# Retention in a two-layer hybrid trunk: chunk states of a head pair as diagonal blocks of a 128-column tile

## The chip, the cores and the metric

The kernel runs on one core of a Trainium2 chip. The metric is device time in microseconds (us). A core has a matrix engine, TensorE (PE), three engines that work on tiles of up to 128 partitions, VectorE (DVE), ScalarE (ACT) and GpSimd (POOL), and SyncE (SP), which here does nothing but issue DMAs. Each engine runs its own list of instructions in order; semaphores tie the lists together.

## The reference

Two layers of a diffusion trunk, 128 context tokens and 1024 latent tokens, width 1024. In each layer one projection feeds four mixers (retention, a Fourier mixer, latent attention, a Hyena convolution), whose outputs go through an output projection and a gated feed-forward network. The change is in the retention of the latent tokens, for four heads with 64 columns each, forward and backward, in chunks of 128 tokens:

```python
scores = jnp.einsum('bnchd,bnmhd->bnhcm', qc, kc) * dmask[None, None]
inner = jnp.einsum('bnhcm,bnmhe->bnche', scores, vc)
kv = jnp.einsum('bnchd,bnche->bnhde', kc * zeta[None, None, :, :, None], vc)
def step(S, kv_j):
    return g_chunk[None, :, None, None] * S + kv_j, S
s_final, s_prev = lax.scan(step, s0, kv)
cross = jnp.einsum('bnchd,nbhde->bnche', qc * xi[None, None, :, :, None], s_prev)
return (inner + cross).reshape(B, L, H, dv), s_final
```

`s_prev` holds the state of a head, 64 x 64, ahead of each chunk. The outputs of both directions are added, normed over a head's 64 columns and gated.

## The kernel before

Tokens lie in nine tiles of 128: eight latent ones and the context. A layer runs in phases: phase 1 (input projection and Hyena), phase 2 (Fourier mixer, retention, attention), phase 3 (output projection), feed-forward network. The layers' phases stand in the trace at about 550 to 840 us (end of phase 1 and phase 2 of layer 0) and 2280 to 2560 us (of layer 1).

A scheduler of the framework sets the order. It takes instructions as their operands and buffers come free, by priorities that the program gives: the Fourier mixer is ahead of the retention's preparation, and the heads' loads of attention are ahead of both. Buffers come from pools. A new pool takes the place of closed pools of an earlier phase, and its first writer waits for the last use there. PSUM, the accumulator memory of PE, is dealt out by tag in phase 2: two banks for transposes (`tr`), three for attention scores (`sc`), one for attention's output (`po`), two for the retention (`r`).

The retention goes through these steps:

- `ret_rope` (L1027) loads the rotation tables (`ropeR`) and q and k of all nine tiles from DRAM (`rqk`, from the projection's output `pj`), and rotates the eight latent tiles on DVE, with two instructions of 128 x 256 and two of 128 x 512 for each tile. The tile of chunk states, `Sall`, serves as scratch.
- `ret_tables` (L977) works out decay masks (`rD`), key scales (`rzt`), chunk decays (`rgt`) and query scales (`rxi`), many small instructions on DVE and ACT.
- `ret_states` (L1042) scales the keys of each tile (`rkz`, DVE), multiplies them with v (`rv`) on PE (L1061, output `pskv`), copies the 64 x 64 blocks on the diagonal into `Sall` (ACT, L1070), and runs the scan: 14 steps of a multiply and an add on DVE, each step on both head pairs at once.
- `ret_tile` (L1080), for each tile: transposes of q and k, scores of the four heads (L1099), their mask (L1100, `rsT`), then the output. For each head (64 columns): one inner product with the 128 rows of `rsT` (L1106) and two cross products, one for each direction, with the 64 rows of the head in `rqx` (scaled q) and `Sall` (L1109). Heads that lie on different halves of the 128 rows write different banks, so there are two output banks and two copies on ACT (L1110).
- `ret_group` (L1112) takes three tiles, then the norm and the gate for all three.

In phase 2 the attention calls `beside` after each pair of query tiles, which runs one step of `ret_group`: retention tiles lie between attention pairs on all engines. An attention pair is: scores on PE (L129 to L131, `sc`), a pass over them on DVE that frees the bank (L903, `pr`), the exponential on ACT (L906), transposes on PE (L917), their split into two parts on ACT and DVE (L120, L125), products with v on PE (L934, L935).

The pools of phase 2, in this order: `rp` (two buffers a tag, for the tiles), `rk` (one buffer, for what lives through the retention: `ropeR`, `Sall`, `rqk`, tables, `rv`), `fp` on the other side of the memory (Fourier), then `at` and `hd` (attention).

Of the kernel before, what the change touches and what calls it, by code (L numbers as in the profile page):

```python
# [10 lines left out]
F32 = mybir.dt.float32  # L11
F32R = mybir.dt.float32r
I32 = mybir.dt.int32
AF = mybir.ActivationFunctionType
ALU = mybir.AluOpType
AX = mybir.AxisListType
PSUM = bass.MemoryType.PSUM
# [18 lines left out]
# ---------------------------------------------------------------- constants of the shapes  # L36
def shape_constants():
# [33 lines left out]
    # channel and position DFTs of the Fourier mixer  # L71
# [10 lines left out]
    # rotary tables, [token of the tile, tile, (first half, second half)]  # L82
# [8 lines left out]
    # retention: distances, masks (with the key scale), positions  # L91
# [7 lines left out]
# ---------------------------------------------------------------- kernel  # L99
class Kern:  # L100
# [12 lines left out]
    # -- small helpers  # L113
# [19 lines left out]
    def rsqrt(self, y, v, pool, tag):  # L133
        """y = v ** -0.5, [p, n]"""
# [20 lines left out]
    # -- two engines for plain arithmetic  # L155
# [13 lines left out]
    # ------------------------------------------------------------ hyena: filters  # L169
    # slots of a tile spectrum (value = re - i * im)  # L170
# [3 lines left out]
    def dft_odd(self, z, d, s, y, tmp):  # L174
        """odd classes from z0, z4 ([p, 1, c]), d, s ([p, 3, c])"""
# [20 lines left out]
    def dft_even_sum(self, a, y, uv, e, s0=8):  # L196
        """classes 0, 8, 4 from a[t] = x[t] + x[t+4]  ([p, 4, c])"""
# [6 lines left out]
    def dft_even_diff(self, b, y, fe, e, s0=8):  # L204
        """classes 2, 6 from b[t] = x[t] - x[t+4]  ([p, 4, c])"""
# [12 lines left out]
    def fft_class(self, r, y, ps, cons, inverse):  # L218
        """ps [p, 2, c]: (re, im) of class r; cons [p, 3, 128]: cos, sin, -sin"""
# [13 lines left out]
    def first(self, n):  # L233
        """what follows n instructions earlier"""
        return self.tc.high_priority(offset=n) if n else nullcontext()

    # ------------------------------------------------------------ modulation rows
# [16 lines left out]
    def ada_steps(self, l, c0, n, pool, psp, tag, dve=(0, 1)):  # L254
        """modulation rows of layer l from column c0 on, n columns at a time, as steps to do beside other work:
        w * silu(c) summed over k-tiles, then over partitions"""
# [40 lines left out]
    # ------------------------------------------------------------ rms norm, modulation, transposition  # L297
    def rstd(self, junk, x, n):
        """1 / sqrt(mean(x^2) + EPS) of [p, n]"""
# [8 lines left out]
    def norm_mod(self, t, x, y, ra, rb, psp, tag, r=None, e="g"):  # L308
        """tile t of the modulated norm of x, transposed and split into T"""
# [21 lines left out]
    # ------------------------------------------------------------ hyena filters  # L331
    def sin_rows(self, v, k, ps, bias, out):
        """out = sin(ps + bias) with the argument brought into [-pi, pi]"""
# [12 lines left out]
    def filter_mlp(self, h1p, h2p, psp, tag):  # L346
        """hidden rows of the filter networks of both layers (64 rows each), to DRAM; the second copy runs backwards"""
# [27 lines left out]
    def filter_spectrum(self, l, o, p1, p2, psp, tag):  # L375
        """spectrum of filter o of layer l, to DRAM"""
# [44 lines left out]
        # the direct term: the filter at distance 0, before the division by the norm  # L421
# [30 lines left out]
    # ------------------------------------------------------------ hyena: long convolution  # L452
    ORDER = (0, 8, 4, 1, 3, 7, 5, 2, 6)

    def spec_mul(self, ps, G, p2):
        """(re, im) of ps * G, values re - i im"""
# [11 lines left out]
    def long_conv(self, l, o, z, gate, p1, p2, psp, tag):  # L468
        """z = gate * conv(z), [p, 9, 256] (tile 8: context); the direct term is part of the filter"""
# [43 lines left out]
        # the parts of the way to the spectrum, and of the way back, in time for the classes that need them  # L513
# [75 lines left out]
    # ------------------------------------------------------------ input projection, hyena, filters  # L589
    WC = 288  # L590

    def w_chunks(self, wp, src, c0, n):
        """weights [p, 8, cols] of columns c0.., four chunks of two k-tiles -> [(hi, lo)] per k-tile"""
# [11 lines left out]
    def hu_block(self, l, b, wp, h1p, sp, psp, ztile, xg):  # L605
        """128 channels of the hyena input: projection, short convolution, back to token rows"""
# [435 lines left out]
    def ret_states(self, l, zt, gt, Sall, keep, psp):  # L1042
# [4 lines left out]
        for d in range(2):  # L1047
            nc.sync.dma_start(Sall[:, 7 * d, :, d], A["sret"][l, :, :, d])
# [817 lines left out]
```

## Time and profile before

| | us |
|---|---|
| median of 3 runs | 3522.32 |
| lowest, highest | 3521.51, 3538.58 |
| profiled execution, its span | 3531.2 |
| PE busy | 3206.7 (91%) |
| DVE busy | 2700.7 (76%) |
| ACT busy | 1286.5 (36%) |
| POOL busy | 1122.7 (32%) |

The profile is of one execution, a little longer than the median. The busy shares are means over stages with different limits, so the stage that a change touches is read by itself: from the table by stretches (busy time of each engine, the granted clock of PE as a share of full speed), from the groups of one tile (count, durations, first and last start) and from the timeline (start, duration, instruction, and in brackets the idle time before it with what ended it). A product in fp32 stands in the trace as two passes. Passes overlap in the pipeline, so their own durations are longer than the distance between starts.

### The profile page before, as it was taken

How to read it: one execution, taken by the hardware profiler on the slowest of the kernel's cores; microseconds unless marked ns; L12 is line 12 of the kernel's file. 1: busy time of each engine (PE TensorE's matmuls, PEld its weight loads, DVE VectorE, ACT ScalarE, POOL GpSimd, SP SyncE). 2: the span in 40 equal slices, each digit the busy share in tenths (PEclk: the TensorE clock that was granted, in tenths of full speed). 3: DMA queues.
4: the chain of work that ended last, by engine and by line, in shares of the span. 5: the costliest groups of instructions: out<-in, count | busy, mean ns of one | idle time of the engine just before them, and what ended most of it. 6: DMA issues, size and time to landing. Idle time of an engine off the chain costs nothing.

```text
span 3531.2 us, 52713 instructions
## 1 busy us (share of the span) xinstructions
PE 3206.7 (91%) x18934; PEld 2830.7 (80%) x18934; DVE 2700.7 (76%) x5024; ACT 1286.5 (36%) x2496; POOL 1122.7 (32%) x947
## 2 busy tenths in 40 slices
PE   8899888999879999989968998899996999999897
PEld 5768777888779999967747787798885999998775
DVE  6676796767898888898897627666788866668898
ACT  3123113545444444443323232254544322223332
POOL 2111430001255555546661014201012422223664
PEclk8899899889989999999987999998898999999998
DMA  5454455104333344343223534531143322213223
GB/s 209 131 168 131 142 157 181 50 17 149 117 111 118 117 129 119 96 134 113 91 88 126 158 108 132 181 106 34 33 165 108 104 74 74 74 58 110 96 72 135
DMA packets 323349, 398.50 MB, mean 113 GB/s; under 512 B 60266, under 2 KB 253543, under 8 KB 322576
## 3 DMA queue, kind: packets, MB, share of 16 engines
q1 hardware_dynamic: 261312, 338.16, 30.1%
q10 hardware_dynamic: 61776, 56.97, 5.2%
q8 instruction: 150, 2.46, 0.3%
q14 instruction: 111, 0.91, 0.1%
HBM read 303.03 MB, written 92.00 MB: 112 GB/s over the span
## 4 chain that ended last, share of the span: by engine, by line
PE 55%; DVE 23%; DMA 6%; issue 6%; POOL 5%; ACT 4%; SPq 0%; ACTq 0%; DVEq 0%; POOLq 0%
PE gu L129 8%; PE gu L131 8%; PE gu L130 8%; DVE ho L125 3%; PE acc L131 3%; PE acc L130 2%; PE acc L129 2%; DMA adw<-in_wada 2%; DVE rq_w L146 2%; DVE acc L157 1%; DVE dw L125 1%; PE pstr L917 1%; DVE adacc L160 1%; POOL acc L157 1%; PE psr L1109 1%
## 5 line engine op out<-in xcount | busy, mean ns | idle before, releaser
L129 PE MATMUL dq<-dw,ho 128*128 128x512 f32 x704 | 289.3, 412 | 47.0 <-DVE acc L157 17.9
L131 PE MATMUL dq<-dw,ho 128*128 128x512 f32 x704 | 289.2, 411 | 34.9 <-DVE ho L125 34.7
L129 PE MATMUL gu<-X,fw 128*128 128x256 f32 x1024 | 290.1, 286 | 7.9 <-ACT fw L120 4.4
L160 DVE SCALAR_TENSOR_TENSOR adacc<-adw,csilu,adacc 128x256 f32<-128x256 f32 x392 | 239.7, 638 | 71.1 <-DMA adw<-in_wada 70.2
L131 PE MATMUL gu<-X,fw 128*128 128x256 f32 x1024 | 287.1, 283 | 1.8 <-DVE fw L125 1.8
L130 PE MATMUL dq<-dw,ho 128*128 128x512 f32 x704 | 287.1, 408 | 0.3 <-DVE dw L125 0.2
L130 PE MATMUL gu<-X,fw 128*128 128x256 f32 x1024 | 285.9, 282 | 0.0
L130 PE MATMUL acc<-wlo,Th 128*128 128x256 f32 (+1 forms) x720 | 217.4, 303 | 5.6 <-DVE wlo L125 5.6
L129 PE MATMUL acc<-whi,Th 128*128 128x256 f32 (+1 forms) x720 | 219.4, 307 | 0.0
L131 PE MATMUL acc<-whi,Tl 128*128 128x256 f32 (+1 forms) x720 | 215.8, 301 | 0.0
L129 PEld LDWEIGHTS dq<-dw,ho 128*128 128x128 f32 x704 | 138.2, 196 | 88.1 <-issue 41.6
L129 PEld LDWEIGHTS gu<-X,fw 128*128 128x128 f32 x1024 | 193.1, 190 | 18.6 <-ACT fw L120 8.1
L131 PEld LDWEIGHTS dq<-dw,ho 128*128 128x128 f32 x704 | 138.1, 196 | 78.3 <-DVE ho L125 45.4
L157 POOL TENSOR_TENSOR adacc<-adacc,adp 128x256 f32<-128x256 f32 x168 | 153.7, 915 | 131.4 <-ACT adp L272 124.4
L131 PEld LDWEIGHTS gu<-X,fw 128*128 128x128 f32 x1024 | 193.3, 190 | 2.3 <-DVE fw L125 2.3
L130 PEld LDWEIGHTS gu<-X,fw 128*128 128x128 f32 x1024 | 193.7, 190 | 0.0
L120 ACT ACTIVATE ho<-hraw 128x384 fp32r<-128x384 f32 (+1 forms) x192 | 87.8, 489 | 272.4 <-POOL hraw L157 254.7
L129 PE MATMUL gu<-x1s,fw 128*128 128x320 f32 x576 | 178.8, 310 | 3.6 <-DVE u L157 3.1
L131 PE MATMUL gu<-x1s,fw 128*128 128x320 f32 x576 | 179.5, 312 | 2.1 <-DVE fw L125 2.0
L130 PE MATMUL gu<-x1s,fw 128*128 128x320 f32 x576 | 179.0, 311 | 0.0
L125 DVE TENSOR_TENSOR ho<-hraw,ho 128x384 fp32r<-128x384 f32 (+1 forms) x192 | 165.6, 879 | 8.1 <-ACT ho L120 8.0
L130 PEld LDWEIGHTS dq<-dw,ho 128*128 128x128 f32 x704 | 138.3, 196 | 32.9 <-DVE dw L125 1.2
(526 smaller groups left out, 10186.7 us busy)
## 6 DMA issues: line engine op xcount, KB each, us to landing
adw<-in_wada SPq DMA_DIRECT2D x320, 128.0 KB
h<-U SPq DMA_DIRECT2D x176, 128.0 KB
X<-in_wf SPq DMA_DIRECT2D x42, 512.0 KB
fr<-in_wf SPq DMA_DIRECT2D x40, 512.0 KB
b<-in_wf SPq DMA_DIRECT2D x24, 768.0 KB
hraw<-h SPq DMA_DIRECT2D x24, 768.0 KB
pj<-pst ACTq DMA_DIRECT2D x90, 128.0 KB
G<-gt SPq DMA_DIRECT2D x36, 256.0 KB
```

Source lines behind the costliest of these rows:

```text
L120: nc.scalar.activation(hi, src, AF.Copy)
L125: (nc.vector if elo == "dve" else nc.gpsimd).tensor_tensor(out=lo, in0=src, in1=hi, op=ALU.subtract)
L129: mm(ps, lh, rh, start=start, stop=False)
L130: mm(ps, lh, rl, start=False, stop=False)
L131: mm(ps, ll, rh, start=False, stop=stop)
L146: nc.vector.scalar_tensor_tensor(out=w, in0=a, scalar=a[:, 0:1], in1=v, op0=ALU.mult, op1=ALU.mult)
L157: (self.nc.vector if e == "v" else self.nc.gpsimd).tensor_tensor(out=out, in0=a, in1=b, op=op)
L160: self.nc.vector.scalar_tensor_tensor(out=out, in0=a, scalar=s, in1=b, op0=op0, op1=op1)
L917: T(pst[:, j], pr[i][:, (k0 + j) * P:(k0 + j + 1) * P], self.ident)
L1109: nc.tensor.matmul(pi[:, pr], qx[q, pr, d], Sall[q, t, pr, d], start=False, stop=d == 1)
```

## The change

The states of a head pair become one 128 x 128 tile: head 0 in the upper left block, head 1 in the lower right, zeros in the other two. `Sall` grows from 64 to 128 columns for each chunk, pair and direction (8 to 16 KB a partition). One cross product then takes all 128 rows of scaled q and gives 128 columns, both heads of a pair; the heads share one output bank, and one copy of 256 columns follows. The zeros are set by two memsets on GpSimd, the loads of the start states go in halves (2 to 4 DMAs a layer), and the scan works on whole 128 x 128 blocks, one instruction for a pair and step (multiply and add in one; 28 a layer as before). To make room, `kvc` and `rv` move from the pool `rk` to tags of `rp` (`rv` gets two buffers, shared with the tiles' `rvg`), and `rot` has two buffers in place of four.

```diff
-        Sall = keep.tile([P, 8, 2, 2, 64], F32, name="Sall")
+        Sall = keep.tile([P, 8, 2, 2, P], F32, name="Sall")
...
-        kvc = keep.tile([P, 2, 2, 64], F32, name="kvc")
+        kvc = pool.tile([P, 4, P], F32, name="kvc", tag="rqkT")[:, 0:2].rearrange("p a (b e) -> p a b e", b=2)
         kzs = keep.tile([P, 2, 2, 4, 64], F32, name="rkz", tag="ropeR")
+        for hh in range(2):
+            nc.gpsimd.memset(Sall[64 * hh:64 * hh + 64, :, :, :, 64 - 64 * hh:P - 64 * hh], 0.0)
         for d in range(2):
-            nc.sync.dma_start(Sall[:, 7 * d, :, d], A["sret"][l, :, :, d])
+            for hh in range(2):
+                q = slice(64 * hh, 64 * hh + 64)
+                nc.sync.dma_start(Sall[q, 7 * d, :, d, q], A["sret"][l, q, :, d])
...
-                v3 = keep.tile([P, 3, 256], F32, name="rv")
+                v3 = pool.tile([P, 3, 512], F32, name="rv", tag="rvg")[:, :, 0:256]
...
-                        nc.scalar.activation(Sall[q, dst, :, d], ps[q, :, d, q], AF.Copy)
+                        nc.scalar.activation(Sall[q, dst, :, d, q], ps[q, :, d, q], AF.Copy)
...
-                tmp = keep.tile([P, 2, 64], F32, name="rst")
-                self.tt("v", tmp, Sall[:, prev, :, d], gt[:, :, d:d + 1].broadcast_to([P, 2, 64]), ALU.mult)
-                self.tt("v", Sall[:, t, :, d], Sall[:, t, :, d], tmp, ALU.add)
+                for k in range(2):
+                    self.stt(Sall[:, t, k, d], Sall[:, prev, k, d], gt[:, k, d:d + 1], Sall[:, t, k, d], ALU.mult, ALU.add)
...
-        for e in range(2):
-            q = slice(64 * e, 64 * e + 64)
-            pi = psp.tile([P, 2, 64], F32, name="psr", tag="r")
-            for pr in range(2):
-                h = 2 * pr + e
-                nc.tensor.matmul(pi[:, pr], sT[:, h], vg[:, 64 * h:64 * h + 64], start=True, stop=not lat)
-                if lat:
-                    for d in range(2):
-                        nc.tensor.matmul(pi[:, pr], qx[q, pr, d], Sall[q, t, pr, d], start=False, stop=d == 1)
-            nc.scalar.activation(o[:, e::2], pi, AF.Copy)
+        pi = psp.tile([P, 4, 64], F32, name="psr", tag="r")
+        for pr in range(2):
+            both = pi[:, 2 * pr:2 * pr + 2].rearrange("p h e -> p (h e)")
+            if lat:
+                nc.tensor.matmul(both, qx[:, pr, 0], Sall[:, t, pr, 0], start=True, stop=False)
+            for h in (2 * pr, 2 * pr + 1):
+                nc.tensor.matmul(pi[:, h], sT[:, h], vg[:, 64 * h:64 * h + 64], start=not lat, stop=not lat)
+            if lat:
+                nc.tensor.matmul(both, qx[:, pr, 1], Sall[:, t, pr, 1], start=False, stop=True)
+        nc.scalar.activation(o, pi, AF.Copy)
...
-            rt = pool.tile([P, 2, P], F32, name="rot", bufs=4)
+            rt = pool.tile([P, 2, P], F32, name="rot")
...
-                self.ret_states(l, zt, gt, Sall, rk, psp)
+                self.ret_states(l, zt, gt, Sall, rk, rp, psp)
```

The scratch of the rotations and tables in `Sall` moves to other chunks of it, since each is now twice as large. The order of the engines changes at the end of phase 1 and in phase 2 of both layers and nowhere else.

SyncE in layer 0, around the load of the rotation tables, before. `fin`, `fch`, `ffc`, `fcons` belong to the Fourier mixer, `rdec` and `rpos` to the decay tables:

```order
L290 DMA mod_5_251<-adw 2x256
L1031 DMA ropeR<-in_ropeR 128x1024
L1153 DMA fin<-pj_97 128x9x256
L1155 DMA fch<-in_chan 128x384
L1157 DMA ffc<-in_fouC 128x256
L1168 DMA fcons<-in_fouF 128x384 x2
L1036 DMA rqk<-pj_97 128x3x512 x3
L981 DMA rdec<-in_rdec 128x8
```

The same place after (`qn` and `kn` are the loads of an attention head):

```order
L1158 DMA fin<-pj_97 128x9x256
L1160 DMA fch<-in_chan 128x384
L1162 DMA ffc<-in_fouC 128x256
L1173 DMA fcons<-in_fouF 128x384 x2
L875 DMA qn<-qd_1250 128x864
L1173 DMA fcons<-in_fouF 128x384 x3
L1031 DMA ropeR<-in_ropeR 128x1024
L1036 DMA rqk<-pj_97 128x3x512 x3
L981 DMA rdec<-in_rdec 128x8
```

`ropeR` has moved behind all Fourier loads. What it waits for has changed too: before, stores and a copy of the Hyena mixer; after, the store and the copy of the last projection group (L732, L733) in layer 0, and in layer 1 those of a group with three still to come. The rest of the queue stands behind it.

DVE in layer 0, the first rotations (`Sall<-rqk,ropeR` and the three after it), before:

```order
L160 SCALAR_TENSOR_TENSOR fin<-fab 128x256 x4
L1188 TENSOR_TENSOR fab<-psx,fq 128x128
L157 TENSOR_TENSOR Sall<-rqk,ropeR 128x8x32 x3
L157 TENSOR_TENSOR rqk<-rqk,ropeR 128x512
L157 TENSOR_TENSOR Sall<-rqk,ropeR 128x8x32
L157 TENSOR_TENSOR rqk<-rqk,Sall 128x512
L1188 TENSOR_TENSOR fab<-psx,fq 128x128
L157 TENSOR_TENSOR rqk<-rqk,ropeR 128x512
```

DVE in layer 0, the end of the rotations and the first score row of attention (`pr,mx<-sc`), after:

```order
L157 TENSOR_TENSOR Sall<-rqk,ropeR 128x8x32
L157 TENSOR_TENSOR rqk<-rqk,Sall 128x512
L157 TENSOR_TENSOR rqk<-rqk,ropeR 128x512
L988 TENSOR_SCALAR rt_5472<-rt_5471 128x8
L997 TENSOR_SCALAR rt_5470<-rdec 128x8
L157 TENSOR_TENSOR rqk<-rqk,Sall 128x512
L989 RECIPROCAL rt_5472<-rt_5472 128x8
L903 TENSOR_SCALAR pr,mx<-sc 128x384
```

Before, the rotations stood between steps of the Fourier mixer, and tables, key scaling and the first scan steps came ahead of the first score row. After, the rotations follow the Fourier mixer as one block and the first score row comes right behind them, the tables (`rt`) beside the score rows, and the key scaling and the scan later, behind two pairs of attention. In layer 1 twelve attention rows stand ahead of the block.

PE in layer 0, the output products of the first retention tile, before:

```order
L1106 MATMUL psr<-rvg,rsT 128x64
L1109 MATMUL psr<-Sall,rqx 128x64 x2
L1106 MATMUL psr<-rvg,rsT 128x64
L1109 MATMUL psr<-Sall,rqx 128x64 x2
L934 MATMUL po<-pth,vhl 128x256
L1106 MATMUL psr<-rvg,rsT 128x64
L1109 MATMUL psr<-Sall,rqx 128x64 x2
L1106 MATMUL psr<-rvg,rsT 128x64
L1109 MATMUL psr<-Sall,rqx 128x64 x2
```

And after:

```order
L1110 MATMUL psr<-Sall,rqx 128x128
L1112 MATMUL psr<-rvg,rsT 128x64 x2
L1114 MATMUL psr<-Sall,rqx 128x128
L1110 MATMUL psr<-Sall,rqx 128x128
L1112 MATMUL psr<-rvg,rsT 128x64 x2
L1114 MATMUL psr<-Sall,rqx 128x128
```

Twelve products of 64 columns have become eight, the four cross ones with 128 columns; each shows as two passes.

## Rows read from the trace of the kernel before

**Rows 1.** The page: span, busy time of engines, one costly group (mean ns).
```profile
span 3531.2 us, 52713 instructions
...
PE 3206.7 (91%) x18934; PEld 2830.7 (80%) x18934; DVE 2700.7 (76%) x5024; ACT 1286.5 (36%) x2496; POOL 1122.7 (32%) x947
...
L160 DVE SCALAR_TENSOR_TENSOR adacc<-adw,csilu,adacc 128x256 f32<-128x256 f32 x392 | 239.7, 638 | 71.1 <-DMA adw<-in_wada 70.2
```

**Rows 2.** Table by stretches: busy time and instructions, then clock and DMA.
```profile
core 0: us, PE busy (x) PEld busy (x) DVE busy (x) ACT busy (x) POOL busy (x), PEclk, DMA share, GB/s
597.00:645.00 48.00, 41.06 (x254) 35.23 (x252) 39.15 (x128) 31.21 (x85) 1.28 (x1) 0.93 0.39 114
645.00:800.00 155.00, 148.51 (x894) 134.71 (x894) 95.27 (x274) 74.67 (x153) 14.81 (x11) 0.82 0.09 24
2280.00:2345.00 65.00, 63.63 (x478) 59.55 (x478) 38.68 (x111) 24.48 (x69) 0.00 (x0) 1.00 0.50 157
2345.00:2384.00 39.00, 37.95 (x283) 35.38 (x281) 31.46 (x104) 25.33 (x64) 1.27 (x1) 1.00 0.33 93
2384.00:2545.00 161.00, 154.00 (x966) 139.98 (x965) 102.79 (x299) 79.95 (x162) 16.28 (x12) 0.86 0.11 30
```

**Rows 3.** Groups of tile psr: ns min/median/max, first and last start.
```profile
L1109 PE MATMUL psr<-Sall,rqx x256: 272/272/473, 645.4 to 2528.8; 64*128 64x64 f32 x128
...
L1087 PE MATMUL psr<-ident,rqk x72: 272/273/273, 635.8 to 2534.2; 128*128 128x128 f32 x72
...
L1110 ACT ACTIVATE ro<-psr x36: 277/278/278, 647.1 to 2537.7; 128x128 f32<-128x128 f32 x36
```

**Rows 4.** Timeline of PE, half of layer 0's first tile: start, duration.
```profile
645.08 0.43 PE L1106 MATMUL psr<-rvg,rsT 128*128 128x64 f32 x2
645.44 0.66 PE L1109 MATMUL psr<-Sall,rqx 64*128 64x64 f32 x4
646.03 0.43 PE L1106 MATMUL psr<-rvg,rsT 128*128 128x64 f32 x2
646.39 0.66 PE L1109 MATMUL psr<-Sall,rqx 64*128 64x64 f32 x4
646.98 0.38 PE L934 MATMUL po<-pth,vhl 128*128 128x256 f32 x1
```

**Rows 5.** Timeline of PE, kv products of layer 0.
```profile
599.68 1.64 PE L1061 MATMUL pskv<-rv,rkz 128*128 128x128 f32 x12
```

**Rows 6.** Timelines of SyncE and of ACT's DMA queue: issues.
```profile
550.94 0.35 SPq L1031 DMA_DIRECT2D ropeR<-in_ropeR  x1
...
556.00 0.40 SPq L1036 DMA_DIRECT2D rqk<-pj  x1
...
596.21 0.33 ACTq L733 DMA_DIRECT2D pj<-pst  x1
...
2342.18 0.33 ACTq L733 DMA_DIRECT2D pj<-pst  x1
```

**Rows 7.** Groups of tiles rqk, Sall and rkz on DVE (both layers).
```profile
L157 DVE TENSOR_TENSOR Sall<-rqk,ropeR x32: 396/414/440, 573.5 to 2302.4; 128x256 f32<-128x256 f32 x32
L157 DVE TENSOR_TENSOR rqk<-rqk,ropeR x16: 674/682/710, 574.5 to 2302.8; 128x512 f32<-128x512 f32 x16
L157 DVE TENSOR_TENSOR rqk<-rqk,Sall x16: 676/682/703, 575.4 to 2303.6; 128x512 f32<-128x512 f32 x16
L157 DVE TENSOR_TENSOR rkz<-rqk,rzt x36: 404/420/426, 599.1 to 2367.4; 128x256 f32<-128x256 f32 x36
L157 DVE TENSOR_TENSOR rst<-Sall,rgt x28: 272/282/837, 598.7 to 2382.5; 128x128 f32<-128x128 f32 x28
```

**Rows 8.** Timelines of DVE and PE: first rotation, rv wait, first score rows.
```profile
573.46 0.77 DVE L157 TENSOR_TENSOR Sall<-rqk,ropeR 128x256 f32<-128x256 f32 x2
...
610.45 4.58 PE L1061 MATMUL pskv<-rv,rkz 128*128 128x128 f32 x24 [2.37 <-DMA rv<-pj]
...
614.72 0.55 DVE L903 TENSOR_SCALAR_CACHE_REDUCE pr<-sc 128x384 f32<-128x384 f32 x1
...
2351.57 0.56 DVE L903 TENSOR_SCALAR_CACHE_REDUCE pr<-sc 128x384 f32<-128x384 f32 x1
```

More of the change, by code (lines that the diff above doesn't have):

```diff
@@ L1010, in ret_tables @@
         nc.scalar.activation(gt, lt, AF.Exp, scale=float(P))
-        scratch = Sall[:, 4:8].rearrange("p t a b c -> p (t a b c)").rearrange("p (n c) -> p n c", c=P)
+        scratch = Sall[:, 4:6].rearrange("p t a b c -> p (t a b) c")
         dist, tm, prow = scratch[:, 0:4], scratch[:, 4:6], scratch[:, 6:8]
@@ L1037, in ret_rope, with ret_states @@
             if t < CTX:
-                tmp = Sall[:, 2 * (t % 2):2 * (t % 2) + 2].rearrange("p a b c d -> p (a b c) d")
+                tmp = Sall[:, t % 2].rearrange("p b c (e d) -> p (b c e) d", d=64)
                 self.rope("v", self.qk[:, t].rearrange("p (h d) -> p h d", h=8), tabs[:, :, t], tmp, 8, 64)
         return Sall
-    def ret_states(self, l, zt, gt, Sall, keep, psp):
+    def ret_states(self, l, zt, gt, Sall, keep, pool, psp):
         nc, A = self.nc, self.A
-        kvc = keep.tile([P, 2, 2, 64], F32, name="kvc")
+        kvc = pool.tile([P, 4, P], F32, name="kvc", tag="rqkT")[:, 0:2].rearrange("p a (b e) -> p a b e", b=2)
         kzs = keep.tile([P, 2, 2, 4, 64], F32, name="rkz", tag="ropeR")
+        for hh in range(2):
+            nc.gpsimd.memset(Sall[64 * hh:64 * hh + 64, :, :, :, 64 - 64 * hh:P - 64 * hh], 0.0)
         for d in range(2):
-            nc.sync.dma_start(Sall[:, 7 * d, :, d], A["sret"][l, :, :, d])
+            for hh in range(2):
+                q = slice(64 * hh, 64 * hh + 64)
+                nc.sync.dma_start(Sall[q, 7 * d, :, d, q], A["sret"][l, q, :, d])
         for t in range(NT):
             if t % 3 == 0:
-                v3 = keep.tile([P, 3, 256], F32, name="rv")
+                v3 = pool.tile([P, 3, 512], F32, name="rv", tag="rvg")[:, :, 0:256]
                 nc.sync.dma_start(v3, self.proj[l][:, t:t + 3, 768:1024])
@@ L1087, in ret_tile @@
             nc.tensor.transpose(ps[:, j], self.qk[:, t, j * P:j * P + P], self.ident)
-        qkT = pool.tile([P, 4, P], F32, name="rqkT")
+        qkT = pool.tile([P, 4, P], F32, name="rqkT", tag="rqkT")
         nc.scalar.activation(qkT, ps, AF.Copy)
@@ L1100, in ret_tile @@
             nc.vector.tensor_tensor(out=sT[:, e::2], in0=pe[e], in1=Dm[:, e::2], op=ALU.mult)
-        for e in range(2):
-            q = slice(64 * e, 64 * e + 64)
-            pi = psp.tile([P, 2, 64], F32, name="psr", tag="r")
-            for pr in range(2):
-                h = 2 * pr + e
-                nc.tensor.matmul(pi[:, pr], sT[:, h], vg[:, 64 * h:64 * h + 64], start=True, stop=not lat)
-                if lat:
-                    for d in range(2):
-                        nc.tensor.matmul(pi[:, pr], qx[q, pr, d], Sall[q, t, pr, d], start=False, stop=d == 1)
-            nc.scalar.activation(o[:, e::2], pi, AF.Copy)
+        pi = psp.tile([P, 4, 64], F32, name="psr", tag="r")
[8 more added lines that the diff above has]
+        nc.scalar.activation(o, pi, AF.Copy)
     def ret_group(self, l, g, Dm, xi, Sall, pool, psp):
         nc = self.nc
-        vg = pool.tile([P, 3, 512], F32, name="rvg")
+        vg = pool.tile([P, 3, 512], F32, name="rvg", tag="rvg")
         o = pool.tile([P, 12, 64], F32, name="ro", bufs=1)
```

## Prediction

> **What bounds the kernel now.** I read the page first: TensorE (PE) is busy for 91% of the span of 3531.2 us, VectorE (DVE) for 76%, ScalarE for 36% [rows 1]. That average says little about the stage that the change touches, so the next view is a table by stretches [rows 2]. In both layers the change lies in the end of phase 1 and in phase 2. In the long middle of phase 2 (645 to 800 us in layer 0, 2384 to 2545 in layer 1) PE is busy for 148.5 of 155 us and 154.0 of 161, DVE for 95.3 and 102.8: PE sets the pace there, and its granted clock is only 0.82 and 0.86 of full speed. In the stretch before (597 to 645) PE has 41.1 of 48 us and DVE 39.2; in layer 1 (2345 to 2384) PE 38.0 of 39 and DVE 31.5. So at the start of phase 2 neither has much room, and in the middle what PE is relieved of is worth its time, until DVE (61 to 64% there) comes close. Before 2345 PE is full (63.6 of 65) and DVE is not (38.7): there DVE work costs nothing.
>
> **The products of a tile.** A latent tile takes 24 passes (an fp32 product shows as two): 8 inner ones with 128 rows and 16 cross ones with 64 rows, both 64 columns wide. In the timeline [rows 4] half a tile runs from 645.08 to 646.98: 1.90 us for 12 passes, 3.80 for a tile. The next work on the list is other work, so this is all that the tile costs PE once its operands are there. After, there are 8 inner and 8 cross passes, 128 rows each, cross 128 columns wide. The nearest row for these is the kv product, 128 rows and 128 columns: 12 passes in 1.64 us [rows 5], and a lone record of that width lasts 0.272 [rows 3], so a pass every (1.64 - 0.27) / 11 = 0.125 us. 16 x 0.125 = 2.0 us, 1.8 less for a tile; 16 latent tiles (8 in each layer) give **-29 us**. Upper bound of the gain: the inner passes, half as wide, at half of it, 16 x 2.3 = -37. Lower bound: nothing, if a 128-column pass costs two of the old ones.
>
> Do two 64-row passes share the array today? The four of one head start at 645.44 and the next product at 646.03, so 0.15 us each, one behind the other [rows 4]. "TensorE: Matmul & The Clock Gate" of the Trainium skill (Part 3, and its table of what to do with small matmuls) says that products on different row groups can run at the same time in the array. By that rule one 128-row product would replace two that might have shared a slot, and the sum would have nothing for the 16 tiles; but the kernel before puts the passes of one row group together, and the rows show no sharing. It is a rival below, with a small chance.
>
> **The clock.** The two stretches with retention tiles run at 0.82 and 0.86, the two stretches of layer 1 before them at 1.00 [rows 2]. Lost against full speed: 155 x 0.18 = 28 us and 161 x 0.14 = 22 us, 50 in all. What differs is that half-filled products stand in the one kind of stretch and not in the other; wide 128-row products replace them. Bounds: -50 if the clock stays at full speed, 0 if it falls as before. I take the half, **-25**: some of the lost cycles lie in the very products that shrink (counted above), and some low stretches follow idle PE, which stays.
>
> **The start of phase 2.** The tile of states (Sall) grows from 8 to 16 KB a partition, and the pool that holds it with the rotation tables (ropeR) and q and k (rqk) can now only be placed on buffers of phase 1. Before, SyncE issued ropeR at 550.94 us and the first rqk at 556.00, and the rotations ran on DVE from 573.46, beside the last projection products [rows 6, 8]. In the new order ropeR stands behind the storing of the last projection group in layer 0, and behind a group with three still to come in layer 1 (that is what its semaphores lead to); everything that SyncE issues later (rqk, decay tables, rv, the next heads' q and k) queues behind it. The groups' stores were issued at 596.21 and 2342.18 [rows 6]. From there to the first rotation: a store, a table, 768 KB of rqk. No row shows this alone; from rqk's issue to the first rotation it was 17.5 us with other work between, which is the upper end, zero the lower; I take 8. The rotations of a layer are 16 x 0.414 + 8 x 0.682 + 8 x 0.682 = 17.5 us of DVE [rows 7], in one block ahead of the first score row of attention in layer 0, and behind a dozen of those in layer 1.
> Layer 0: 596 + 8 + 17 = 621 us for the first score row, against 614.72 before [rows 8], 6 late. The kv products that PE did before 614.72 now come behind two pairs of attention, some 48 of 72 passes at 0.137 [rows 5], another 7: **+13**. Layer 1: 2342 + 8 = 2350, when the projection ends too; the first score row came at 2351.57 before [rows 8] and comes about then again, a dozen such rows take 5 us, and then the 17 us of rotations hold back all others. PE has scores and transposes for some 5 of these: **+12**. Bounds for a layer: +5 (only the wait, with attention work beside the rotations) and +35 (wait, rotations and a third of the next block with an idle PE).
>
> **Tables, states, scan.** The table arithmetic moves between attention rows, where DVE has room. The key scaling (18 x 0.42 = 7.6 us) and the scan (28 x 0.282 = 7.9) [rows 7] stood among the attention rows; in the new order the scan is one unbroken block ahead of the first tile. The instructions stay 28, now a scalar-tensor-tensor of 128 x 128; the nearest row is 128 x 256 at 0.638 [rows 1], half of that 0.32, so 1 us more a layer. While the block runs no score leaves its bank; PE has kv products and transposes for part of it. Between 0 and 16 us a layer, I take 5: **+10**. Costed at nothing: the two memsets on GpSimd, hidden by the rotations' wait and the key scaling, which come first (uncovered, they would hold the scan back by some us); two more DMAs for the start states, beside the same work; ScalarE's copy of the output, one of 256 columns for two of 0.278 [rows 3], on an engine that is 36% busy; rot with two buffers for four, where ScalarE waits for a store at each third copy; rv with two buffers, which takes away the wait of 2.37 us at 610.45 [rows 8] at best.
>
> **Sum.** -29 - 25 + 25 + 10 = -19 us. The profiled execution is 3531.2 us, the median of the shown runs 3522.32; 3531.2 - 19 = 3512, times 3522.32 / 3531.2 gives **3503 us**. About 0.5% (17.6 us) is what a measurement of this kernel can tell from no change, so the forecast stands on that edge.
>
> **Rivals.** (A) The clock stays up and the attention pairs that now come first cover the scan: -29 - 50 + 25 = -54, 3468. For it: full clock wherever the half-filled products are missing [rows 2]. Against: PE idles at the start, and DVE has at least 20 us more in phase 2. (B) Slower: the chain store, table, rqk, rotations, scan becomes the path of both layers, 8 + 17.5 + 10 = 35 us each, PE idle beside it, and what follows runs at DVE's pace, so of the clock only 10 come back: 70 - 29 - 10 = +31, 3553. It decides once a layer's start costs over (29 + 25) / 2 = 27. For it: in layer 1 the rotations were free before 2345, and now no engine has room; against: attention needs none of rqk, and its loads are on SyncE ahead of it. (C) The clock falls as before, since PE waits more often: -29 + 35 = +6, 3528, no change. (D) The products don't get cheaper (a 128-column pass at two old ones; the rule above): 0 - 25 + 35 = +10, 3532.
>
> **Chances.** Forecast 0.33, A 0.19, B 0.20, C 0.23, D 0.05. The forecast's own spread (3490 to 3515) puts some two thirds of it past 0.5%: faster 0.22 + 0.19 = 0.41, same 0.11 + 0.23 + 0.05 = 0.39, slower 0.20. The range reaches to A and to B, 3468 to 3552, which leaves the outer halves of both, under 0.2; the forecast's own is 3490 to 3515.
>
> **What would show it.** In the profile of the changed kernel: a half tile's passes in about 1.0 us; a granted clock over 0.9 in the middle of phase 2; the first rotation at about 604 us and the first score row at about 621 in layer 0; PE idle for some 13 us more between 597 and 660, and as much in layer 1; DVE 75 to 85% busy in the middle. The forecast is wrong if PE keeps its low clock (C), if DVE has no gaps for 60 us after the rotations (B), or if the start is no later than before (A).

## The result and the profile after

The changed kernel takes 3512.1 us (median of 6 runs, 3505.88 to 3516.0); the kernel before, run beside it, takes 3529.64 (6 runs). The ratio of the runs is 0.9944, with a 95% interval of 0.9926 to 0.9962: 20 us faster. The forecast was 3503 against a median of 3522.32, a ratio of 0.9945.

The page of the changed kernel, its span and busy times:

```profile
span 3510.3 us, 52487 instructions
...
PE 3150.4 (90%) x18806; PEld 2777.8 (79%) x18806; DVE 2693.1 (77%) x5024; ACT 1286.0 (37%) x2478; POOL 1131.5 (32%) x951
```

The busy shares hardly moved, though two things of about 40 and 60 us happened, in opposite directions. The table by stretches shows them (busy time of each engine, then granted clock, DMA share and GB/s, as in [rows 2]):

```profile
597.00:645.00 48.00, 25.59 (x146) 22.64 (x144) 37.09 (x123) 20.11 (x45) 0.00 (x0) 0.72 0.44 134
645.00:800.00 155.00, 141.75 (x1030) 127.74 (x1030) 123.58 (x378) 94.87 (x202) 24.55 (x15) 0.97 0.19 50
2280.00:2345.00 65.00, 64.41 (x475) 60.04 (x475) 17.26 (x48) 21.22 (x49) 0.00 (x0) 1.00 0.37 118
2345.00:2384.00 39.00, 22.66 (x137) 19.95 (x136) 36.28 (x117) 18.43 (x50) 0.00 (x0) 0.74 0.29 81
2384.00:2545.00 161.00, 150.01 (x1083) 135.77 (x1082) 129.93 (x401) 98.93 (x204) 22.81 (x16) 0.97 0.20 59
```

In the two middle stretches the granted clock is 0.97 where it was 0.82 and 0.86, and DVE is busy for 80% of the time where it was 61 to 64%: the same attention work passes faster. In the two starting stretches it is the other way: PE is busy for 25.6 us of 48 (41.1 before) and 22.7 of 39 (38.0), at a clock of 0.72 and 0.74. And DVE does 17.3 us of work beside the end of layer 1's projection (2280 to 2345) where it did 38.7.

What the start looks like in layer 0, on SyncE, DVE and PE (start, duration, instruction, in brackets the idle time before it and what ended that):

```profile
598.38 0.33 SPq L1031 DMA_DIRECT2D ropeR<-in_ropeR  x1
598.76 0.43 SPq L1036 DMA_DIRECT2D rqk<-pj  x1
```
```profile
606.10 1.10 DVE L157 TENSOR_TENSOR Sall<-rqk,ropeR 128x256 f32<-128x256 f32 x3 [7.34 <-issue]
...
622.09 0.51 DVE L903 TENSOR_SCALAR_CACHE_REDUCE pr<-sc 128x384 f32<-128x384 f32 x1
```
```profile
602.62 0.64 PE L1205 MATMUL psx<-fx,fch 128*128 128x128 f32 x2
622.66 0.69 PE L129 MATMUL sc<-at_Tl,at_Th 96*128 96x384 f32 x1 [19.40 <-DVE pr L903]
...
663.64 0.69 PE L1110 MATMUL psr<-Sall,rqx 128*128 128x128 f32 x2
```

The rotation tables are asked for 47 us later than before [rows 6], the first rotation runs at 606.1 (573.5 before, [rows 8]), the first score row at 622.1 (614.7), and PE stands still for 19.4 us until that row frees a bank. The first cross product comes at 663.6, against 645.4 [rows 4].

And the products, half of a later tile of layer 0:

```profile
717.17 0.39 PE L1110 MATMUL psr<-Sall,rqx 128*128 128x128 f32 x2
717.39 0.56 PE L1112 MATMUL psr<-rvg,rsT 128*128 128x64 f32 x4
717.78 0.44 PE L1114 MATMUL psr<-Sall,rqx 128*128 128x128 f32 x2
717.98 0.42 PE L129 MATMUL sc<-at_Tl,at_Th 96*128 96x384 f32 x1
```

Eight passes from 717.17 until the next work at 717.98, 0.81 us, for twelve in 1.90 [rows 4].

For all kernels below I give one more reading of the trace, since the profiled executions reach phase 2 at different times (up to 12 us apart in layer 0, more in layer 1): the time from the start of the last projection pass (`acc`) to the first cross product, and from there to the first pass of the output projection (`wo`), for layer 0 / layer 1. Ratios are to the kernel before, run on the same chip. Where the text compares two ratios, the "give or take" behind the difference is worked out from their two intervals as if they were independent.

| kernel | to the first cross product, us | from there to the output projection, us | ratio (95%) |
|---|---|---|---|
| before | 50.0 / 34.3 | 198.1 / 193.5 | 1 |
| changed | 69.1 / 60.8 | 167.5 / 163.8 | 0.9944 (0.9926 to 0.9962) |
| old_products_late | 71.9 / 63.3 | 199.1 / 196.7 | 1.0117 (1.0097 to 1.0136) |
| old_products_rot2_early | 49.8 / 36.1 | 201.7 / 200.7 | 1.0030 (1.0016 to 1.0044) |
| new_products_early | 53.8 / 39.5 | 162.8 / 164.4 | 0.9835 (0.9820 to 0.9850) |
| old_products_new_states | 52.4 / 38.7 | 199.4 / 199.6 | 1.0035 (1.0015 to 1.0055) |
| two_banks_128_rows | 51.0 / 39.2 | 179.5 / 176.9 | 0.9916 (0.9889 to 0.9942) |
| split_128_rows | 50.8 / 38.9 | 175.3 / 175.7 | 0.9885 (0.9861 to 0.9910) |
| late_low_priority | 68.0 / 59.8 | 162.8 / 165.6 | 0.9949 (0.9932 to 0.9966) |
| early_low_priority | 49.1 / 37.0 | 166.4 / 164.0 | 0.9839 (0.9804 to 0.9874) |
| late_no_rotation | 58.6 / 52.4 | 167.8 / 157.4 | 0.9915 (0.9888 to 0.9943) |
| early_no_rotation | 46.3 / 37.6 | 161.8 / 165.3 | 0.9842 (0.9815 to 0.9870) |
| early_rot4 | 50.4 / 39.9 | 158.7 / 160.0 | 0.9837 (0.9811 to 0.9863) |
| early_rot4_low_priority | 47.7 / 38.4 | 156.5 / 157.3 | 0.9823 (0.9798 to 0.9848) |

The changed kernel loses 19.1 + 26.5 = 46 us ahead of the first cross product and gains 30.6 + 29.7 = 60 us behind it. That places 14 of the 21 us by which the two profiled executions differ; the rest is spread over stages whose order of work did not change.

### The profile page after: what moved, and what is told of

It is laid out like the page before. It is cut to its first block, busy times and chain, and to the rows that moved or that the text cites. A ratio compares the mean times of both kernels' runs of the same rounds, so it can differ in the third digit from the quotient of the medians.

```text
span 3510.3 us, 52487 instructions
## 1 busy us (share of the span) xinstructions
PE 3150.4 (90%) x18806; PEld 2777.8 (79%) x18806; DVE 2693.1 (77%) x5024; ACT 1286.0 (37%) x2478; POOL 1131.5 (32%) x951
## 4 chain that ended last, share of the span: by engine, by line
PE 47%; DVE 28%; DMA 8%; issue 6%; POOL 6%; ACT 4%; SPq 0%; DVEq 0%; ACTq 0%; POOLq 0%
PE gu L129 7%; PE gu L131 7%; PE gu L130 7%; DMA adw<-in_wada 4%; DVE ho L125 3%; PE acc L130 3%; PE acc L129 3%; PE acc L131 2%; DVE adacc L160 2%; DVE rq_w L146 2%; DVE acc L157 1%; PE dq L131 1%; PE dq L129 1%; DVE dw L125 1%; DMA G<-gt 1%
```

## Experiments: the start and the products taken apart

**old_products_late** is the kernel before with one edit:

```diff
-            rt = pool.tile([P, 2, P], F32, name="rot", bufs=4)
+            rt = pool.tile([P, 2, P], F32, name="rot")
```

> The kernel before with one edit: rot gets two buffers in place of four. That makes the pool ahead of rk 2 KB smaller, so that ropeR lies on a buffer of the last projection groups and is loaded as late as in the changed kernel (in both layers); the products and the states are those of before. Theory 1 (the late start and the new products are two separate terms, and the start costs about 16 us a layer, as the delay of the first cross product in the changed kernel's trace: 645.4 to 663.6 us in layer 0, 2384.1 to 2397.6 in layer 1): 25 to 35 us slower than before, about 3560. Theory 2 (the start costs nothing, since the attention rows that now come first fill it, and the -20 us of the change is the products' alone): within 5 us of before.

3574.74 us, ratio 1.0117. Theory 1 said 3560, so it holds in sign and is too small in size. The trace has the same start as the changed kernel's, from an edit that has nothing to do with the states:

```profile
603.31 0.33 SPq L1031 DMA_DIRECT2D ropeR<-in_ropeR  x1
603.69 2.29 SPq L1036 DMA_DIRECT2D rqk<-pj  x3
```

The pool `rp` is 2 KB smaller, so `ropeR`, the first tile of the next pool `rk`, lies 2 KB lower (bytes 126080 to 130176 of a partition, for 128128 to 132224), and the top 2 KB of the projection's staging tiles (`pst`) reach to 127104. One KB of overlap makes the load wait for the projection. (These are the addresses of the built kernels, not of a trace.) In the changed kernel `ropeR` has the same lower address, 126080: `rv` and `kvc` took buffers of `rp` that were there before, and the larger `Sall` lies behind `ropeR`, so it is the two buffers of `rot` that moved it.

**new_products_early** turns that around for the changed kernel:

```diff
+            self.rd = c.enter_context(tc.tile_pool(name="rd", bufs=1, reuse_waits="tile"))
             rk = c.enter_context(tc.tile_pool(name="rk", bufs=1, reuse_waits="tile"))
...
-        Dm = pool.tile([P, 4, P], F32, name="rD")
+        Dm = self.rd.tile([P, 4, P], F32, name="rD")
```

> The changed kernel with one edit: the decay masks rD get a pool of their own, 2 KB, ahead of rk. ropeR lies 2 KB higher, off the last projection groups' buffers, and is loaded as early as in the kernel before; products, states and scan are those of the change. Theory 1: the start's 25 to 35 us come back, about 3482, 45 to 55 us under before. Theory 2: as the changed kernel, about 3510.

3474.06 us, ratio 0.9835: theory 1, and theory 2 falls. The masks, which are needed late, now lie on the staging tiles, and the tables are loaded early again. Against the changed kernel the ratio differs by 0.0109, 38 us (give or take 8).

**old_products_rot2_early** puts the same pool into old_products_late, so what is left of the difference from before is the two buffers of `rot` and the new place of the masks.

> The kernel before with rot in two buffers, as in old_products_late, and the decay masks in a pool of their own ahead of rk, as in new_products_early: ropeR is early again. If where ropeR lies is all that old_products_late lost: within 5 us of the kernel before. If two buffers for rot cost by themselves (ScalarE waiting for a store at each third copy), which would be part of what old_products_new_states lost: 5 to 15 us slower than before.

3538.25 us, ratio 1.0030 with an interval that leaves out 1: the late start of old_products_late was worth 0.0087, 31 us (give or take 8), and the two buffers, with the masks moved, 10 us (give or take 5). What ScalarE waits for the buffers is small, though. In the groups of tile `rot` over both layers:

```profile
  DMA mixR<-rot: 2.9, 2
```

Two waits, 2.9 us in all, which don't occur in the kernel before. The rest is not found; the order of the attention passes around the transposes differs as well.

So the late start costs 31 us with the old products and 38 with the new, which the noise does not tell apart. The rest of the change, without it, is worth 0.9835, 58 us.

## Experiments: what the products gain

All three have the early start and the new states, and differ only in the products.

**old_products_new_states** has the products of before, read out of the diagonal blocks:

```diff
-                nc.tensor.matmul(both, qx[:, pr, 0], Sall[:, t, pr, 0], start=True, stop=False)
...
+                        nc.tensor.matmul(pi[:, pr], qx[q, pr, d], Sall[q, t, pr, d, q], start=False, stop=d == 1)
```

> new_products_early with the products of before (64 rows, 64 columns, read out of the diagonal blocks, two banks, two copies). The states' preparation (memset, block copies, scan in one instruction a step and pair, pools) is the new one, the start is early. If the preparation is neutral: within 6 us of before, clock about 0.82 to 0.86 in the middle of phase 2. If it costs (the scan as one block): 5 to 15 us slower than before. If it gains: faster than before by as much, and the products are worth less than new_products_early shows.

3540.87 us, ratio 1.0035, the same as old_products_rot2_early (1.0030). So memsets, block copies and the one-instruction scan cost nothing that shows beside the two buffers of `rot` (2 us, give or take 9).

**split_128_rows** gives each cross product 64 columns again but all 128 rows:

```diff
-                nc.tensor.matmul(both, qx[:, pr, 0], Sall[:, t, pr, 0], start=True, stop=False)
...
+                        nc.tensor.matmul(pi[:, h], qx[:, pr, d], Sall[:, t, pr, d, cs], start=False, stop=d == 1)
```

> new_products_early with the cross products cut into two of 64 columns each, all 128 rows: 24 passes for a latent tile as before, but none with 64 rows; one bank and one copy. If the gain of the products is the number of passes (8 fewer for each of 16 tiles at 0.125 us, and the clock follows from that), it gives back 16 to 29 us of new_products_early. If it is the rows (no change between 64 and 128 rows between neighbours, and a clock that stays up), it gives back under 10 us and the granted clock in the middle of phase 2 stays over 0.95.

3490.59 us, ratio 0.9885: 18 us more than new_products_early (give or take 10), 53 us less than old_products_new_states (give or take 11). The expectation had these as alternatives, and both are at work: 8 more passes for each of 16 tiles cost 18 us, and the rows are worth three times that at the same number of passes.

**two_banks_128_rows** keeps the two banks, the two copies and the order by halves too, and differs from old_products_new_states in the rows alone:

```diff
-                        nc.tensor.matmul(pi[:, pr], qx[q, pr, d], Sall[q, t, pr, d, q], start=False, stop=d == 1)
+                        nc.tensor.matmul(pi[:, pr], qx[:, pr, d], Sall[:, t, pr, d, q], start=False, stop=d == 1)
```

> old_products_new_states with one difference: the cross products take all 128 rows of scaled q and 64 columns of the block tile (the other head's rows meet zeros); order by halves, two banks and two copies stay as in old_products_new_states. If it is the 64 rows that cost (change of rows between neighbours, half-filled passes and the clock): as split_128_rows, 3485 to 3500, with a clock over 0.93 from the first cross product on. If it is the two banks, the two copies or the order of heads: near old_products_new_states, 3530 to 3545.

3492.59 us, ratio 0.9916: 42 us for the rows by themselves (give or take 12). From split_128_rows, with its one bank, one copy and other order, it is not told apart. It multiplies the other head's 64 rows by zeros, twice the arithmetic, and is faster. The timelines of one half tile tell a part of it. old_products_new_states, 12 passes in 657.60 to 659.40:

```profile
657.60 0.33 PE L1111 MATMUL psr<-rvg,rsT 128*128 128x64 f32 x2
657.87 0.66 PE L1114 MATMUL psr<-Sall,rqx 64*128 64x64 f32 x4
658.45 0.43 PE L1111 MATMUL psr<-rvg,rsT 128*128 128x64 f32 x2
658.82 0.66 PE L1114 MATMUL psr<-Sall,rqx 64*128 64x64 f32 x4
659.40 0.38 PE L934 MATMUL po<-pth,vhl 128*128 128x256 f32 x1
```

split_128_rows, 12 passes in 650.98 to 652.30, with 128 rows throughout:

```profile
650.98 0.39 PE L1110 MATMUL psr<-rvg,rsT 128*128 128x64 f32 x2
651.21 0.61 PE L1113 MATMUL psr<-Sall,rqx 128*128 128x64 f32 x4
651.65 0.39 PE L1110 MATMUL psr<-rvg,rsT 128*128 128x64 f32 x2
651.88 0.61 PE L1113 MATMUL psr<-Sall,rqx 128*128 128x64 f32 x4
652.30 0.42 PE L129 MATMUL sc<-at_Tl,at_Th 96*128 96x384 f32 x1
```

new_products_early, 8 passes in 648.60 to 649.42:

```profile
648.60 0.39 PE L1110 MATMUL psr<-Sall,rqx 128*128 128x128 f32 x2
648.83 0.56 PE L1112 MATMUL psr<-rvg,rsT 128*128 128x64 f32 x4
649.22 0.44 PE L1114 MATMUL psr<-Sall,rqx 128*128 128x128 f32 x2
649.42 0.42 PE L129 MATMUL sc<-at_Tl,at_Th 96*128 96x384 f32 x1
```

Where 128 and 64 rows follow each other, the step costs more: from 658.45 to 658.82 for two inner passes, against 651.65 to 651.88. Read pass by pass over both layers, where the clock is full and no pass waits, the median distance of starts is 0.11 us between two passes of 64 rows and between two of 128, and 0.20 us where the one kind follows the other. A half tile takes 1.80 us (1.90 in the kernel before [rows 4]), 1.32 and 0.82. By 32 half tiles that is 15 to 19 us for the rows and 16 for the passes. Sixteen agrees with the 18 measured. For the rows 42 to 53 were measured, so some 23 to 38 are left, and the clock is what else differs. Table by stretches, from the first cross product to the output projection in layer 0 and layer 1, first old_products_new_states, then two_banks_128_rows, then new_products_early:

```profile
657.90:857.30 199.40, 184.90 (x1179) 167.78 (x1178) 137.55 (x391) 107.97 (x213) 17.74 (x13) 0.87 0.16 49
2398.50:2598.10 199.60, 185.08 (x1179) 167.96 (x1178) 137.97 (x391) 107.54 (x213) 17.72 (x13) 0.87 0.17 49
```
```profile
650.50:829.90 179.40, 164.31 (x1178) 149.73 (x1178) 136.98 (x391) 106.86 (x213) 17.74 (x13) 0.94 0.18 54
2376.90:2553.70 176.80, 161.96 (x1178) 147.46 (x1177) 138.14 (x392) 107.79 (x214) 17.72 (x13) 0.96 0.18 55
```
```profile
647.20:810.00 162.80, 150.24 (x1118) 136.44 (x1116) 131.97 (x392) 105.85 (x204) 17.73 (x13) 0.99 0.20 60
2359.70:2524.10 164.40, 152.46 (x1117) 139.22 (x1115) 132.40 (x392) 105.97 (x204) 17.73 (x13) 0.97 0.20 59
```

The clock is 0.87 with 64 rows, 0.94 and 0.96 with 128, at an equal number of passes. Against full speed the first loses 0.13 of 199.4 us in each layer, 52 in all, the second some 18: an estimate of 34 us for the clock, which overlaps a little with the 15 to 19, since some of the slow steps lie in slow stretches. PE is not idler in the first (93% busy in both layers, 92% in the second), so idle time is not what lowers the clock there; the 64-row cross products are, the one thing that the edit changes. Whether it is the unused rows or the longer steps around them is not told apart.

## Experiments: what the late start costs

**late_low_priority** is the changed kernel with the retention's preparation at attention's own priority:

```diff
-            with tc.high_priority(offset=100):
+            with tc.high_priority(offset=0):
                 Sall = self.ret_rope(l, rk)
```

> The changed kernel with one edit: rotations, tables and states at attention's own priority, not ahead of it. ropeR still waits for the last projection groups (late start), but on DVE the rotations stand between score rows, one to four at a time, and not in one block ahead of them. If the late start costs because the block keeps the scores from leaving their banks while PE has nothing else: 15 to 25 us faster than the changed kernel, 3487 to 3497, and the 19 us gap of PE ahead of the first pass that follows it falls to under 8. If it costs because everything behind the states comes later: as the changed kernel, 3505 to 3515.

3508.97 us, ratio 0.9949, the same as the changed kernel (2 us slower, give or take 9), so the 15 to 25 us that I expected are not there. The gap that I had named shrank as I had said:

```profile
615.91 0.69 PE L129 MATMUL sc<-at_Tl,at_Th 96*128 96x384 f32 x1 [4.61 <-DVE pr L903]
...
670.85 0.46 PE L1110 MATMUL psr<-Sall,rqx 128*128 128x128 f32 x2 [1.42 <-issue]
```

4.6 us in place of 19.4. But this is a weaker test of the theory than I meant it to be. The table by stretches from the last projection pass to the first cross product, layer 0 and layer 1, shows PE's idle time as a whole (the length less the first busy time); first new_products_early, then the changed kernel, then late_low_priority:

```profile
593.40:647.20 53.80, 45.79 (x264) 39.65 (x262) 41.34 (x135) 32.37 (x87) 6.05 (x3) 0.84 0.41 118
2320.20:2359.70 39.50, 35.70 (x236) 31.72 (x234) 35.27 (x109) 25.31 (x67) 4.87 (x3) 0.91 0.39 109
```
```profile
594.60:663.60 69.00, 40.27 (x244) 35.36 (x244) 55.20 (x180) 32.74 (x87) 8.29 (x3) 0.78 0.47 141
2336.80:2397.60 60.80, 40.88 (x263) 36.36 (x262) 56.26 (x183) 29.70 (x80) 5.07 (x3) 0.83 0.42 128
```
```profile
602.90:670.90 68.00, 49.58 (x279) 39.63 (x277) 55.51 (x180) 34.43 (x90) 5.04 (x3) 0.80 0.47 144
2335.10:2394.90 59.80, 40.25 (x267) 35.92 (x265) 55.59 (x180) 30.75 (x82) 5.10 (x3) 0.86 0.42 131
```

With the late start PE is idle for 28.7 and 19.9 us there, against 8.0 and 3.8: 37 us more, as much as the late start costs. late_low_priority leaves 18.4 and 19.6. It took away 10.3 us in layer 0 and 0.4 in layer 1; there the rotations still stand on DVE in one block (2343.8 to 2358.2), and PE's gap of 14.6 us beside it is as in the changed kernel. The first cross product comes no earlier in either layer: 68.0 us after the projection's last pass (69.1 in the changed kernel), and 59.8 (60.8). So the run shows that lower priority does not help and that closing one gap of 19 us is worth nothing that shows; it does not show that PE's idle time costs nothing.

**early_low_priority** has the same edit on new_products_early.

> new_products_early with the same edit as late_low_priority: here the rotations still fall beside the projection, and the edit only lets score rows of attention between the scan steps. If the scan's nearly unbroken block costs what old_products_new_states lost against the kernel before (about 10 us): 3 to 10 us faster than new_products_early, 3464 to 3471. If not: within 3 us of it.

3469.72 us, ratio 0.9839 against 0.9835: no difference, but one that is only known to 13 us either way. By itself this run can't exclude that the scan's block costs the 10 us that I gave it; old_products_new_states (2 us, give or take 9, for all of the states' preparation) speaks against it.

**late_no_rotation** leaves out the rotation of q and k for seven of eight latent tiles of the changed kernel, and **early_no_rotation** that of new_products_early:

```diff
-                self.rope("v", ...)
+                if t == 0: self.rope("v", ...)
```

> The changed kernel with work left out: q and k of seven of the eight latent tiles are not rotated (the first is). ropeR, rqk and all that follows are loaded as late as in the changed kernel; DVE is spared 7/8 of 17.5 us in each layer. If the late start costs because that DVE work no longer lies beside the projection: 25 to 35 us faster than the changed kernel, 3477 to 3487. If it costs because the data come late (store, tables, rqk, rv one after the other): under 12 us faster, over 3500.

> The same work left out of new_products_early, where the rotations lie beside the projection. If they are hidden there: within 5 us of new_products_early (3474). If not, up to 30 us faster.

late_no_rotation: 3497.68 us, ratio 0.9915, 10 us under the changed kernel's 0.9944, give or take 12: the 25 to 35 us of the first theory are not there, but what the rotations do cost is not clear of the noise. early_no_rotation: 3468.95, ratio 0.9842, no difference from new_products_early, give or take 11. In the trace of late_no_rotation the first cross product comes 10.5 and 8.4 us earlier than in the changed kernel. The two kernels of this pair differ in the start alone, with 7/8 of the rotations (31 us of DVE work) left out of both, and still by 0.0073, 26 us (give or take 14). So by the middle values most of what the late start costs does not need the rotations. What is left of it then is the data's lateness: tables, q and k, then v, one behind the other on SyncE, and kv products, scan and tiles behind these. Which link of that chain weighs most was not tried by itself.

## Experiments: a faster version

**early_rot4** gives `rot` four slots in the place of the rotation tables, with `rxi` in the masks' pool, and **early_rot4_low_priority** adds the lower priority:

```diff
+            self.rots = rk.tile([P, 4, 2, P], F32, name="rots", tag="ropeR")
...
-            rt = pool.tile([P, 2, P], F32, name="rot")
+            rt = self.rots[:, (3 * g + j) % 4]
...
-        xi = pool.tile([P, 2, 2, P], F32, name="rxi")
+        xi = self.rd.tile([P, 2, 2, P], F32, name="rxi")
```

> new_products_early with four buffers for rot again: four slots of one tile that takes the place of the rotation tables and scaled keys once these are done; the query scales go into the decay masks' pool, so that ropeR stays where it is. If two buffers for rot cost 10 us in any order (as old_products_rot2_early against the kernel before): about 3464, 10 us under new_products_early. If the 10 us were the old products' alone (order of the half-filled passes, clock), which the new products don't have: within 4 us of new_products_early.

> early_rot4 and the lower priority of early_low_priority together. If both help by themselves: 3458 to 3462. If neither does: within 4 us of new_products_early.

3466.56 us, ratio 0.9837, and 3462.34 us, ratio 0.9823 (0.9798 to 0.9848). The first is the same as new_products_early, give or take 11: with the new products no cost of the two buffers for `rot` shows, but the 10 us that they cost with the old ones are not excluded either. new_products_early and these two are 57 to 62 us faster than before and some 40 us faster than the changed kernel; among themselves they are not told apart.

## Why the prediction was right, point by point

- **The sum was right, in part by luck.** Forecast: -54 for the products and the clock, +35 for the start and the states, -19. Measured: -58 (new_products_early against before) and +38 (the changed kernel against new_products_early), -20. The halves are not cut quite alike: the -58 has the states and the two buffers of `rot` in it, the +38 is the start alone. Inside both halves terms were mis-sized, and the errors cancel.
- **Products, -29.** The half tile takes 0.82 us, 0.103 a pass instead of the 0.125 taken, so 35 us over 32 half tiles at full clock. The inner passes of 64 columns are the shorter ones: the upper bound (-37) was nearer.
- **The clock, -25, half of what was lost.** The cause given held: two_banks_128_rows shows that the 64-row products lower the clock and that 128 rows bring most of it back. The half did not hold as a reading of the clock: in the two middle stretches the changed kernel loses 155 x 0.03 + 161 x 0.03 = some 10 us against full speed, where 50 were lost before. But 35 for the passes and 40 for the clock are more than the 60 us gained behind the first cross product, so the two overlap, as the prediction said of the cycles in the very products that shrink. With 35 for the passes 23 of the 58 are left for the clock: a remainder, near the 25, not a measurement.
- **The row-group rule.** The Trainium skill's page "TensorE: Matmul & The Clock Gate", Part 3, says that products on different row groups can run at the same time. In the kernel before the cross products of the two halves never follow each other directly, and the passes show none of it: they start 0.11 us or more apart, one behind the other. Rival D falls by the half tile, eight passes in 0.81 us. Products of both halves side by side were not tried.
- **The start, +25, and the scan, +10.** The first steps of the chain came out as worked out: first rotation at 606.1 (604 forecast), first score row at 622.1 (621). The idle time that follows was taken too small. Between 597 and 660 us PE is idle for 27.2 us where it was 7.2, 20 more (13 forecast), and in layer 1, from the last projection pass to the first cross product, for 19.9 where it was 1.0, 19 more (12 forecast). The late start costs 31 to 38, not 25. The scan costs nothing that shows (old_products_new_states), not 10. That the two sum to the forecast 35 is luck. The price was put down to the block of rotations, with PE idle behind it; the added idle time is there, 37 us against new_products_early, but with 7/8 of the rotations left out the late start still costs 26 (give or take 14), so by the middle values the lateness of the data weighs more than the block.
- **Why the start is late.** I put it down to the larger tile of states. It is the pool ahead: `rot` in two buffers alone, without any change to the states, has the same effect (old_products_late). An address that moved by 2 KB did it.
- **Costed at nothing.** `rot` in two buffers shows no cost in the changed kernel (early_rot4, give or take 11), but 10 us in the kernel before. Memsets and start-state loads show none together with the scan (old_products_new_states). The single copy and the two buffers of `rv` were not tried by themselves.
- **Rivals.** A had both its conditions: the clock stayed up (0.97), and the scan shows no cost. Its price of -54 did not come out, since it added passes and clock in full and took the start at 25; that an early start gives -58 is another sum with a similar result. B's threshold (27 us a layer) was not reached: 38 for both layers. C falls by the clock, 0.97.

## What to carry to other kernels

A product with half of the array's rows may be worth padding with zeros where wide products stand next to it: here twice the arithmetic on the same number of passes gained 42 us, by estimate 15 to 19 of it by shorter steps and the rest with the clock. When an edit changes the size of a pool, look at which tile of the next pool comes to lie on a buffer that is freed late, and put a tile there that is written late: 2 KB moved cost 31 to 38 us, and a reordering of pools gave it back. And after filling an engine's idle gap, add up all its idle time again, in every layer: closing the largest gap, of 19 us, gained nothing that shows here, with 38 us of idle time left where there had been 49.

## What the runs showed of the hardware that was not expected

PE's granted clock depends on what the products use, not only on whether PE is busy: at 93% busy it was 0.87 with 64-row cross products among the others, and at 92% busy, with as many passes, 0.94 and 0.96 with 128-row ones (two_banks_128_rows). A change between 64 and 128 rows has a price at full clock, too: 0.20 us to the next pass, where equal neighbours take 0.11. And a pause costs beyond its length. In the changed kernel the granted clock right behind the idle 19.4 us is half of full speed (1.2 of 2.4 GHz), and a few microseconds later it is full; the table by stretches over 623 to 629 and 630 to 636 us:

```profile
623.00:629.00 6.00, 5.90 (x18) 5.36 (x18) 5.09 (x25) 2.70 (x4) 0.00 (x0) 0.50 0.01 2
630.00:636.00 6.00, 6.00 (x44) 5.68 (x42) 5.34 (x22) 4.87 (x9) 0.00 (x0) 1.00 0.02 4
```

PE is busy for all but 0.1 us of both, with 18 passes in the first (scores only) and 44 in the second (scores and others).
